# Moving the positions' load to SyncE's queue, and putting the lambda vectors into a buffer of the first chunks

## The chip, the cores and the metric

The kernel runs on one core of a Trainium2 chip. The metric is the device time of one execution in microseconds (us), taken as the median of several runs. The engines of the core are PE (TensorE, matrix products; its weight loads are listed apart as PEld), DVE (VectorE), ACT (ScalarE), POOL (GpSimd) and SP (SyncE, which here only issues DMAs). DMAs can also be issued by ACT and POOL. A queue name such as SPq means the instruction stream of that engine as far as it issues DMAs.

## The reference

One decoder layer on 512 tokens of width 1024, in float32. Cut to what the change is near:

```python
def reference(x, mem, positions, g_mix, w_in, lambda_q1, lambda_k1, lambda_q2, lambda_k2, ...):
    cos, sin = rope_tables(positions, x.dtype)      # angles = positions * 8 frequencies
    u = rms_norm(h, g_mix[l]) @ w_in[l]             # 512 x 1024 @ 1024 x 3072: q, k, v of two mixers
    qa = apply_partial_rope(qa, cos, sin)
    ka = apply_partial_rope(ka, cos, sin)
    lam = (exp(sum(lambda_q1 * lambda_k1)) - exp(sum(lambda_q2 * lambda_k2)) + lam_init)
    ya = diff_attention(qa, ka, va, lam, g_subln[l], lam_init)      # softmax 1 - lam * softmax 2
    yb = stick_breaking_attention(qs, ksb, vs)
    h = h + concatenate([ya, yb]) @ w_out[l]
    h = h + cross_attention(rms_norm(h, g_cross), rms_norm(mem, g_mem), w_xq, w_xkv, w_xo)
    h = h + square(relu(rms_norm(h, g_mlp) @ w_up)) @ w_down
    return rms_norm(h, g_final)
```

The positions feed the rotary tables; the four lambda vectors of 64 numbers feed one scalar, `lam`, that is first used in the softmax of the first mixer.

## The kernel before

Every float32 product is made of three products of halves: each operand is split into `hi` (rounded) and `lo` (the rest), and `mm3` (lines 101 to 104) adds hi·hi, hi·lo and lo·hi in one PSUM tile. ACT makes a `hi` (lines 109, 111), DVE the `lo` (lines 113, 115), for the weights as for the activations. PE is fed by a static order of products that is written out by hand; the other loads and splits are placed around it.

The change touches the start, about the first 36 us. There the input `x` comes in four column blocks `xt[0..3]`, and each of its eight chunks of 128 columns goes through `first_chunk(c)`: PE transposes it into PSUM (line 544), ACT and DVE split it into `A[0][:, c]` and `A[1][:, c]` (lines 111 and 115; the trace calls them `a`). `first_mm(w, c)` then multiplies chunk c with the first 512 columns of `w_in`, into four PSUM tiles (`sc`, `av`), 12 products for each chunk. The loop `for c in range(2, 8, 2)` goes over pairs of chunks. Inside it, `load_x` issues the next block of x on SP, `keep_x` copies the transposed chunks to SBUF on ACT (line 555) and stores them to HBM on SP (line 556), `fetch` issues the next weight load on SP (line 122), and `squares(c)` sums the squares of one block: ACT squares it into `junk`, which has two buffers used in turn (line 572), and DVE reduces that (line 573). In the last round, c = 6, `means` makes of these sums the scale of each token with a chain of tiny DVE instructions of four elements a partition (lines 577 to 582 and, through `rsqrt`, 170 to 175), and chunk 7's `lo` (line 115) stands behind that chain on DVE.

Two small side jobs run beside this. The positions are loaded by POOL (line 532); POOL converts them (line 647) and reduces the angles in a chain of 34 small instructions (lines 649 to 665), ACT takes the sines (lines 668, 669), DVE spreads them (lines 672 to 684) and PE transposes the tables (line 693). The four lambda vectors, each broadcast to 128 partitions of 256 bytes, are loaded by SP into `lv` (line 635); DVE multiplies and sums them (lines 704, 706), ACT takes the exponentials (line 707) and DVE makes `neglam` (lines 708, 709).

The order on PE, and in this part on ACT and DVE, is the one in which the code is written, except that what is written behind `order.close()` (line 697; the lambda arithmetic is) is placed by a scheduler where it expects the inputs. SP's and POOL's order is the scheduler's. Each engine then works strictly in order. DMAs of SP and ACT take eight completion semaphores in turn, so that a DMA also waits for the one that had its semaphore before.

Of the kernel before, what the change touches and what calls it, by code (L numbers as in the profile page):

```python
# [10 lines left out]
F32 = mybir.dt.float32  # L11
# [7 lines left out]
P = 128  # L19
# [43 lines left out]
def tile_decoder_layer(  # L63
# [24 lines left out]
    nc = tc.nc  # L88
# [52 lines left out]
    def fetch(n):  # L141
        while len(loaded) < min(len(stream), n):
            loaded.append(stream[len(loaded)]())

    def take(ahead=2):
        fetch(taken[0] + 1 + ahead)
        taken[0] += 1
        return loaded[taken[0] - 1]
# [39 lines left out]
    def tr_tile():  # L188
        return pp.tile([P, S], F32, tag="tr", bufs=2, name="tr")
# [329 lines left out]
    sp = st.enter_context(tc.tile_pool(name="st", bufs=1))  # L519
# [8 lines left out]
    def load_x(c):  # L528
        nc.sync.dma_start(xt[c], x[:, c * 256:(c + 1) * 256].rearrange("(t p) d -> p t d", p=P))

    pos_i = sp.tile([P, 4], I32, name="pos_i")
    nc.gpsimd.dma_start(pos_i, positions[0].rearrange("(t p) -> p t", p=P))
    lv = sp.tile([P, 4, 64], F32, name="lv")

    qs = [q_tiles() for _ in range(4)] + [None] * 4
    ks = [None] * 8
# [4 lines left out]
    def first_chunk(c):  # L541
        ps = mm_tile() if c % 2 else tr_tile()
        for t in range(4):
            nc.tensor.transpose(ps[:, t * P:(t + 1) * P], xt[c // 2][:, t, (c % 2) * P:(c % 2 + 1) * P], ident)
        split(A[0][:, c, :], A[1][:, c, :], ps, gcol[:, c:c + 1])

        x_ps[c] = ps
# [4 lines left out]
    def keep_x(c):  # L552
        xs = sp.tile([P, 2, S], F32, tag="xs", bufs=2, name="xs")
        for i in range(2):
            nc.scalar.copy(xs[:, i, :], x_ps[c + i])
        nc.sync.dma_start(xdram[:, c:c + 2, :], xs)

    def first_mm(w, c):
        if c < 2:

            for a, b in ((0, 0), (0, 1), (1, 0)):
                for h in range(4):
                    nc.tensor.matmul(q_ps[h], w[a][:, c, h * P:(h + 1) * P], A[b][:, c, :],
                                     start=c == 0 and a + b == 0, stop=False)
            return
        for h in range(4):
            col = slice(h * P, (h + 1) * P)
            mm3(q_ps[h], (w[0][:, c % 2, col], w[1][:, c % 2, col]), (A[0][:, c, :], A[1][:, c, :]), c == 0, c == 7)

    def squares(c):  # L570
        junk = sp.tile([P, 4, 256], F32, tag="junk", bufs=2, name="junk")
        nc.scalar.activation(junk, xt[c], AF.Square, bias=0.0, scale=1.0)
        nc.vector.tensor_reduce(ss4[:, c, :], junk, AX.X, ALU.add)

    def means():
        ss = sp.tile([P, 4], F32, name="ss")
        nc.vector.tensor_reduce(ss, ss4.rearrange("p c t -> p t c"), AX.X, ALU.add)
        nc.vector.tensor_scalar(ss, ss, 1.0 / D, EPS, ALU.mult, ALU.add)
        r = rsqrt(sp, ss, 4, "rsx")
        nc.vector.tensor_copy(rs, r)  # L580
        nc.vector.tensor_scalar(rs8, r, 0.125, None, ALU.mult)
        nc.vector.tensor_scalar(nrs8, r, -0.125, None, ALU.mult)
# [24 lines left out]
    for c in range(2, 8, 2):  # L607
        if c == 4:
            tr = tr_tile()
            nc.tensor.transpose(tr[:, 0:25], grow, ident[:25, :25])  # L610
            nc.vector.tensor_copy(gcol[:, 8:33], tr[:, 0:25])
            nc.vector.tensor_scalar(gcol[:, 32:33], gcol[:, 32:33], 1.0 - LAM_INIT, None, ALU.mult)
        load_x(c // 2)
        keep_x(c - 2)
        fetch(c // 2 + 1)
        w = take(0)
        if c == 2:
            first_mm(w, 0)
        if c == 6:
            squares(2)  # L620
            first_chunk(6)
            squares(3)
            means()
            first_chunk(7)
        else:
            first_chunk(c)
            squares(c // 2 - 1)
            first_chunk(c + 1)
        if c > 2:
            first_mm(w, c - 2)  # L630
        first_mm(w, c - 1)
    keep_x(6)
    w = take(0)
    for i, v in enumerate((lambda_q1, lambda_k1, lambda_q2, lambda_k2)):
        nc.sync.dma_start(lv[:, i, :], v.broadcast_to([P, 64]))
    fetch(5)
# [696 lines left out]
```

## Time and profile before

| | |
|---|---|
| median of 3 runs | 780.06 us (779.12 to 781.5) |
| the profiled execution, its own time | 783.51 us |
| its span in the trace | 781.7 us |
| granted TensorE clock, mean | 0.993 of full speed |
| PE busy in the span | 763.2 us, 98% |
| DVE busy | 516.6 us, 66% |
| ACT busy | 424.8 us, 54% |
| POOL busy | 74.7 us, 10% |

Between the span and the execution's own time lie 1.8 us. The trace gives for each instruction its start, its duration and what its engine waited for before it, in us from the span's start; for a DMA it gives the time at which the issuing engine was busy with it and, apart from that, how long after the issue the data had landed. PE is in work nearly all the time, so what counts is where PE stands idle.

### The profile page before, as it was taken

Reading aid. Unit: us, or ns where it says so; the run is one execution under the profiler, and the core shown is the slowest. Engines: PE = TensorE matmul, PEld = TensorE weight load, DVE = VectorE, ACT = ScalarE, POOL = GpSimd, SP = SyncE. Lnnn points to the kernel's source line nnn. Section 1 sums busy time; section 2 is a strip of 40 time slices with the busy share of each in tenths; the row PEclk is TensorE's granted clock in tenths of the full one; section 3 lists DMA queues with packets and bytes.
Section 4 is the critical chain, followed back from the end, with each engine's and each line's share of the span. In section 5 each row is a group of like instructions: output and inputs, shape, how many; then the busy total and the mean of one; then the engine's idle time right before and its main releaser. Section 6 shows DMA issues by size and latency. Waiting matters only on the chain.

```text
span 781.7 us, 11806 instructions
## 1 busy us (share of the span) xinstructions
PE 763.2 (98%) x4618; PEld 662.0 (85%) x4618; DVE 516.6 (66%) x809; ACT 424.8 (54%) x720; POOL 74.7 (10%) x196
## 2 busy tenths in 40 slices
PE   8999999999898999999999999999999999999996
PEld 7787988778767898888788999889988899889885
DVE  4796665686766664465656989547855586647745
ACT  6657565886845543453535886334733364444622
POOL 6242332311000020000000030000000000000000
PEclk9999999999998999999999999999999999999999
DMA  8466363766643454241560145241333233220302
GB/s 289 162 144 142 82 147 90 169 136 134 182 142 120 124 162 135 80 135 55 162 189 1 51 166 158 81 139 54 109 103 112 81 109 109 99 91 1 135 1 107
DMA packets 88425, 91.61 MB, mean 117 GB/s; under 512 B 3473, under 2 KB 71730, under 8 KB 88114
## 3 DMA queue, kind: packets, MB, share of 16 engines
q1 hardware_dynamic: 84528, 78.39, 32.0%
q0 software_dynamic: 3200, 11.54, 8.1%
q10 hardware_dynamic: 642, 0.93, 0.3%
q8 instruction: 36, 0.59, 0.3%
q14 instruction: 19, 0.16, 0.1%
HBM read 73.03 MB, written 4.19 MB: 99 GB/s over the span
## 4 chain that ended last, share of the span: by engine, by line
PE 87%; ACT 5%; DVE 3%; DMA 3%; issue 2%; POOL 0%; DVEq 0%; SPq 0%; POOLq 0%; ACTq 0%
PE mm L102 14%; PE mm L103 14%; PE mm L104 14%; PE av L102 5%; PE av L104 5%; PE av L103 5%; PE sc L102 4%; PE sc L104 4%; PE sc L103 4%; PE tr L103 4%; PE tr L104 4%; PE tr L102 4%; PE sc L385 2%; PE tr L428 1%; PE av L457 1%
## 5 line engine op out<-in xcount | busy, mean ns | idle before, releaser
L113 DVE TENSOR_TENSOR lo<-raw,hi 128x1024 fp32r<-128x1024 f32 (+1 forms) x73 | 88.2, 1209 | 41.1 <-ACT hi L109 39.9
L109 ACT ACTIVATE hi<-raw 128x1024 fp32r<-128x1024 f32 (+1 forms) x73 | 76.2, 1045 | 63.9 <-PE tr L103 15.2
L109 ACT ACTIVATE hi<-blk 128x1024 fp32r<-128x1024 f32 x40 | 42.5, 1061 | 70.1 <-PE sc L104 48.3
L102 PE MATMUL mm<-a,hi 128*128 128x512 f32 x152 | 64.1, 422 | 3.5 <-DVE resid L493 3.2
L113 DVE TENSOR_TENSOR lo<-blk,hi 128x1024 fp32r<-128x1024 f32 x40 | 48.8, 1221 | 25.9 <-ACT hi L109 25.9
L104 PE MATMUL mm<-a,lo 128*128 128x512 f32 x152 | 61.1, 402 | 0.1
L103 PE MATMUL mm<-a,hi 128*128 128x512 f32 x152 | 61.0, 401 | 0.0
L102 PE MATMUL mm<-b,hi 128*128 128x512 f32 x128 | 50.3, 393 | 0.0
L104 PE MATMUL mm<-b,lo 128*128 128x512 f32 x128 | 50.0, 391 | 0.0
L103 PE MATMUL mm<-b,hi 128*128 128x512 f32 x128 | 49.9, 390 | 0.0
L104 PE MATMUL av<-a,lo 128*128 128x256 f32 (+1 forms) x140 | 41.0, 293 | 0.0
L102 PE MATMUL av<-a,hi 128*128 128x256 f32 (+1 forms) x140 | 40.9, 292 | 0.0
L103 PE MATMUL av<-a,hi 128*128 128x256 f32 (+1 forms) x140 | 40.9, 292 | 0.0
L102 PEld LDWEIGHTS mm<-a,hi 128*128 128x128 f32 x152 | 29.3, 193 | 9.6 <-DVE resid L493 3.7
L102 PE MATMUL tr<-a,hi 128*128 128x256 f32 x128 | 36.2, 283 | 0.0
L104 PE MATMUL tr<-a,lo 128*128 128x256 f32 x128 | 36.2, 283 | 0.0
L103 PE MATMUL tr<-a,hi 128*128 128x256 f32 x128 | 36.2, 283 | 0.0
L104 PEld LDWEIGHTS mm<-a,lo 128*128 128x128 f32 x152 | 29.2, 192 | 7.3 <-DVE lo L113 0.5
L103 PEld LDWEIGHTS mm<-a,hi 128*128 128x128 f32 x152 | 29.4, 194 | 5.6 <-DVE a L113 0.2
L102 PE MATMUL mm<-hi,a 128*128 128x256 f32 x112 | 33.1, 295 | 0.0
L109 ACT ACTIVATE hi<-s 128x1024 fp32r<-128x1024 f32 x16 | 17.0, 1061 | 27.3 <-PE sc L104 14.6
L104 PE MATMUL mm<-hi,a 128*128 128x256 f32 x112 | 31.6, 282 | 0.0
(404 smaller groups left out, 2349.1 us busy)
## 6 DMA issues: line engine op xcount, KB each, us to landing
blk<-in_w_up_dram SPq DMA_DIRECT2D x32, 512.0 KB, 3.7
raw<-in_w_down_dram SPq DMA_DIRECT2D x32, 512.0 KB, 3.2
raw<-in_w_in_dram SPq DMA_DIRECT2D x23, 512.0 KB, 4.5
lo<-raw POOLq DMA_DIRECT2D x20, 512.0 KB, 4.8
raw<-in_w_xkv_dram SPq DMA_DIRECT2D x16, 512.0 KB, 3.8
raw<-in_w_out_dram SPq DMA_DIRECT2D x8, 512.0 KB, 4.6
raw<-in_w_xq_dram SPq DMA_DIRECT2D x8, 512.0 KB, 3.9
raw<-in_w_xo_dram SPq DMA_DIRECT2D x8, 512.0 KB, 4.3
```

Of the source, the lines that this page charges most:

```text
L102: nc.tensor.matmul(o, l[0], r[0], start=first, stop=False)
L103: nc.tensor.matmul(o, l[0], r[1], start=False, stop=False)
L104: nc.tensor.matmul(o, l[1], r[0], start=False, stop=last)
L109: nc.scalar.activation(hi, src, AF.Copy, bias=0.0, scale=scale)
L113: (eng or nc.vector).tensor_tensor(lo, src, hi.bitcast(F32), ALU.subtract)
L385: nc.tensor.matmul(sc[:, h, :n], q[a][own[h], blk], k[b][own[h], :n], start=n_pass == 0, stop=False)
L428: nc.tensor.transpose(tr[:, j, :], self.es[i][:, h, j * P:(j + 1) * P], ident)
L457: nc.tensor.matmul(o[:, cols], vj, w, start=(j == 0 and part == 0), stop=(j == 3 and part == 1))
```

## The change

Two loads are moved; nothing that is computed changes.

```diff
     pos_i = sp.tile([P, 4], I32, name="pos_i")
-    nc.gpsimd.dma_start(pos_i, positions[0].rearrange("(t p) -> p t", p=P))
-    lv = sp.tile([P, 4, 64], F32, name="lv")
...
         if c == 6:
+            nc.sync.dma_start(pos_i, positions[0].rearrange("(t p) -> p t", p=P))
             squares(2)
             first_chunk(6)
             squares(3)
...
     keep_x(6)
     w = take(0)
+    lv = sp.tile([P, 4, 256], F32, tag="junk", bufs=2, name="lv")[:, :, 0:64]
     for i, v in enumerate((lambda_q1, lambda_k1, lambda_q2, lambda_k2)):
         nc.sync.dma_start(lv[:, i, :], v.broadcast_to([P, 64]))
```

The positions (512 integers, 4 bytes to a place) are now loaded by SP. The lambda vectors now lie in the `junk` buffer that `squares(2)` used, so their loads wait for DVE's reduction of that buffer. In the changed kernel line numbers from 534 to 619 are smaller by two, those from 620 to 633 by one, and those behind are the same.

On SP, at the place of the lambda loads, the order before was (in brackets what an instruction waits for: an engine's semaphore, or one of the DMA semaphores HW0 to HW7):

```order
L529 DMA x_117<-in_x_dram 128x4x256 [waits DMAHW5_49]
L635 DMA lv<-in_lambda_q_dram 128x64 [waits DMAHW6_49]
L635 DMA lv<-in_lambda_k_dram 128x64 [waits DMAHW7_49]
L635 DMA lv<-in_lambda_q_dram 128x64 [waits DMAHW0_49]
L635 DMA lv<-in_lambda_k_dram 128x64 [waits DMAHW1_49]
L122 DMA raw<-in_w_in_dram 128x2x512 [waits DMAHW2_49,DVE_49]
L556 DMA xdram<-xs 128x1024 [waits DMAHW3_49,Activation_49]
```

Now the positions stand behind the last block of x:

```order
L529 DMA x_117<-in_x_dram 128x4x256 [waits DMAHW5_49]
L618 DMA pos_i<-in_positions_dram 128x4x1 [waits DMAHW6_49]
L122 DMA raw<-in_w_in_dram 128x2x512 [waits DMAHW7_49,DVE_49]
L554 DMA xdram<-xs 128x1024 [waits DMAHW0_49,Activation_49]
L122 DMA raw<-in_w_in_dram 128x8x128 [waits DMAHW2_49,DMAHW1_49,DVE_49]
```

And the lambda loads stand four weight loads and three stores later on SP, behind the weights for the first `v` columns:

```order
L554 DMA xdram<-xs 128x1024 [waits Activation_49]
L122 DMA raw<-in_w_in_dram 128x4x256 [waits DMAHW7_49,DMAHW5_49,DVE_49]
L635 DMA lv<-in_lambda_q_dram 128x64 [waits DMAHW6_49,DVE_49]
L635 DMA lv<-in_lambda_k_dram 128x64
L635 DMA lv<-in_lambda_q_dram 128x64 [waits DMAHW0_49]
L635 DMA lv<-in_lambda_k_dram 128x64 [waits DMAHW1_49]
L554 DMA xdram<-xs 128x1024 [waits DMAHW2_49,Activation_49]
```

The positions have taken the first place of the lambda loads, and these wait for DVE now. On DVE, the chain of `means` stood alone before (`ss`, `rsx`, `rsx_t` are its tiles):

```order
L170 TENSOR_SCALAR rsx<-ss 128x4 [waits DVE_49]
L172 TENSOR_TENSOR rsx_t<-rsx 128x4 [waits DVE_49]
L174 SCALAR_TENSOR_TENSOR rsx_t<-rsx_t,ss 128x4 [waits DVE_49]
L175 SCALAR_TENSOR_TENSOR rsx<-rsx_t,rsx 128x4 [waits DVE_49]
L172 TENSOR_TENSOR rsx_t<-rsx 128x4 [waits DVE_49]
```

Now the lambda arithmetic stands inside it:

```order
L170 TENSOR_SCALAR rsx<-ss 128x4 [waits DVE_49]
L172 TENSOR_TENSOR rsx_t<-rsx 128x4 [waits DVE_49]
L704 TENSOR_TENSOR lp<-lv 128x128 [waits DMAHW6_49,DMAHW7_49,DMAHW1_49,DMAHW0_49]
L174 SCALAR_TENSOR_TENSOR rsx_t<-rsx_t,ss 128x4 [waits DVE_49]
L706 TENSOR_REDUCE ls<-lp 128x2 [waits DVE_49]
L175 SCALAR_TENSOR_TENSOR rsx<-rsx_t,rsx 128x4 [waits DVE_49]
L172 TENSOR_TENSOR rsx_t<-rsx 128x4 [waits DVE_49]
L708 TENSOR_TENSOR neglam<-ls 128x1 [waits Activation_49]
L174 SCALAR_TENSOR_TENSOR rsx_t<-rsx_t,ss 128x4 [waits DVE_49]
L709 TENSOR_SCALAR neglam<-neglam 128x1 [waits DVE_49]
L175 SCALAR_TENSOR_TENSOR rsx<-rsx_t,rsx 128x4 [waits DVE_49]
```

Four instructions have moved in from earlier places, and the first of them waits for the four lambda loads. Behind this piece, unchanged, come one more round of lines 172 to 175, three copies and chunk 7's `lo`. On ACT the exponential of line 707 moves from before the copies of chunks 4 and 5 to between those of chunks 6 and 7. On POOL the load is gone and the chain is otherwise the same; PE's order is the same throughout.

## Rows read from the trace of the kernel before

**Rows 1.** The page, busy us (share of the span) xinstructions.

```profile
PE 763.2 (98%) x4618; PEld 662.0 (85%) x4618; DVE 516.6 (66%) x809; ACT 424.8 (54%) x720; POOL 74.7 (10%) x196
```

**Rows 2.** Waits of PE, whole span: us in total, times, longest.

```profile
PE mm L102 <- DVE resid L493: 3.2, 1, 3.2
...
PE mm L544 <- DMA x<-in_x_dram: 0.5, 1, 0.5
```

**Rows 3.** DMA issues: KB each, us from issue to landing.

```profile
x<-in_x_dram SPq DMA_DIRECT2D x1, 256.0 KB, 3.0
...
x<-in_x_dram SPq DMA_DIRECT2D x1, 256.0 KB, 5.3
...
lv<-in_lambda_k_dram SPq DMA_DIRECT2D x1, 32.0 KB, 7.1
```

**Rows 4.** Stretches: PE, PEld, DVE, ACT, POOL busy, PEclk, DMA share, GB/s.

```profile
5.00:6.00 1.00, 1.00 (x7) 0.94 (x7) 0.17 (x1) 0.00 (x0) 0.00 (x0) 1.00 0.72 108
6.00:7.00 1.00, 0.59 (x6) 0.32 (x3) 0.19 (x1) 0.91 (x2) 0.00 (x0) 1.00 0.67 161
...
9.00:10.00 1.00, 1.00 (x6) 0.82 (x5) 0.90 (x2) 0.99 (x3) 0.91 (x2) 1.00 1.06 388
```

**Rows 5.** Timeline of POOL: start, us, engine, line, operation [idle before <-releaser].

```profile
2.14 0.99 POOL L532 DMA_DIRECT2D pos_i<-in_positions_dram  x1
...
7.67 0.54 POOL L647 CAST pos<-pos_i 128x4 f32<-128x4 int32 x1 [3.47 <-DMA pos_i<-in_positions_dram]
...
12.28 1.28 POOL L658 TENSOR_TENSOR ang<-ang,kp 128x32 f32<-128x32 f32 x1
...
16.23 0.25 POOL L658 TENSOR_TENSOR ang<-ang,kp 128x32 f32<-128x32 f32 x1
...
22.41 0.29 POOL L665 TENSOR_SCALAR anc<-anc 128x32 f32<-128x32 f32 x1
```

**Rows 6.** Timeline of SP.

```profile
7.51 1.13 SPq L635 DMA_DIRECT2D lv<-in_lambda_q_dram  x1
8.69 0.43 SPq L635 DMA_DIRECT2D lv<-in_lambda_k_dram  x1
...
24.04 0.38 SPq L122 DMA_DIRECT2D raw<-in_w_in_dram  x1
```

**Rows 7.** Timeline of DVE.

```profile
12.23 1.23 DVE L113 TENSOR_TENSOR lo<-raw,hi 128x1024 fp32r<-128x1024 f32 x1 [2.33 <-ACT hi L109]
...
16.24 0.39 DVE L704 TENSOR_TENSOR lp<-lv 128x128 f32<-128x128 f32 x1 [0.25 <-DMA lv<-in_lambda_q_dram]
...
16.67 0.29 DVE L706 TENSOR_REDUCE ls<-lp 128x2 f32<-128x128 f32 x1
...
23.93 1.21 DVE L573 TENSOR_REDUCE ss<-junk 128x4 f32<-128x1024 f32 x1
...
27.59 0.16 DVE L172 TENSOR_TENSOR rsx_t<-rsx 128x4 f32<-128x4 f32 x1
27.78 0.16 DVE L174 SCALAR_TENSOR_TENSOR rsx_t<-rsx_t,ss 128x4 f32<-128x4 f32 x1
...
29.58 0.74 DVE L115 SCALAR_TENSOR_TENSOR a<-mm,gcol,a 128x512 fp32r<-128x512 f32 x1
...
33.95 0.18 DVE L672 TENSOR_TENSOR cs<-cs,rs 128x32 f32<-128x32 f32 x1
...
35.38 0.17 DVE L682 COPY ctok<-cs 128x32 f32<-128x32 f32 x1
```

**Rows 8.** The chain that ended last, 10 to 35 us: start, us, what.

```profile
30.98 0.23 PE sc L103
```

**Rows 9.** Timeline of PE's weight loads.

```profile
35.60 0.58 PEld L693 LDWEIGHTS tr<-ident,ctok 128*128 128x128 f32 x4
```

**Rows 10.** Timeline of ACT and its queue.

```profile
11.13 1.06 ACT L109 ACTIVATE hi<-raw 128x1024 fp32r<-128x1024 f32 x1 [1.14 <-DMA raw<-in_w_in_dram]
...
33.35 0.21 ACT L669 ACTIVATE cs<-anc 128x32 f32<-128x32 f32 x1
```

## Prediction

> **What bounds the kernel now.** I read the page first: PE is busy for 763.2 of 781.7 us [rows 1], so a change counts only where it makes PE wait or ends a wait. The waits of PE come next: the longest, 3.24 us, is late in the first half and has nothing to do with the two loads; the only one at the start that the list shows is 0.54 us for a block of x [rows 2]. Then I looked for what stands closest behind PE where the moved instructions now are: the chain that ended last runs through PE there, product after product. In it the first product with chunk 7's lo begins at 30.98 us [rows 8]. That lo is made by DVE at 29.58 and takes 0.74 us, so it is there at 30.32 [rows 7]: **PE has 0.66 us in hand**. A second place is a little later. The cosine is done on ACT at 33.56 [rows 10], DVE takes it up at 33.95 and ends the cosine table with the instruction from 35.38 to 35.55 [rows 7], and PE loads the first piece of it at 35.60 [rows 9]. So ACT has 0.39 us in hand there, and DVE none worth counting. ACT's chain to the cosine hangs on DVE as well: its copy of chunk 7 waits for that same lo, and a split, a table load and the sine follow in order.
>
> **The load leaves POOL.** POOL loses an issue of 0.99 us [rows 5]; nothing waits for POOL there, and POOL then waits 3.47 us for the data anyway, so the issue itself is worth nothing. What may be worth something is the traffic. While the positions' load is on its way, until 7.67 us, the DMA engines move 108 and 161 GB/s from 5 to 7 us, against 388 from 9 to 10 [rows 4]; the second half of the first x block needs 5.3 us to land, the first half 3.0 [rows 3]. Missing are (388 - 108) + (388 - 161) = 507 GB/s times 1 us, about 0.5 MB or 1.3 us of full rate. Some of that is there because SP itself waited before the next x block; how much is due to the positions the trace doesn't tell. What can be gained is bounded by two waits: PE's 0.54 us [rows 2] and ACT's 1.14 us for the weights at 11.13 [rows 10]. So between 0 and 1.0 us, PE's own work between them taking some; I take the middle, **0.5 us gained**.
>
> **The load arrives on SP.** It takes the first place of the lambda loads, at about 7.5 us. Its issue there costs nothing to what is queued behind it on SP: one issue takes the place of four, so the next weight load can only come earlier. The lambda load at 8.69 landed after 7.1 us, at 15.8 [rows 3, 6], behind the same queue of x and weights, and I give the positions the same time. 512 places of 4 bytes have no row of their own; the range goes from 14.6 (7.51 + 7.1) to 20 us. POOL then starts 8.1 us later than at 7.67; its chain took 15.03 us to 22.70 [rows 5], with stretched instructions beside lo splits in it (one in rows 5), and lo splits lie in the new stretch too. So it ends near **30.9 us**. The sine and cosine were taken at 33.2 to 33.6 [rows 10], so the tables are in time by 2.5 us, and by more if ACT is late itself. Cost 0 as long as the positions land before 18.3 us.
>
> **But the chain now runs beside other work.** Before, POOL was done when the chain of tiny DVE instructions began. What happens when both read SBUF shows at 12.28: an instruction of POOL that takes 0.25 us elsewhere took 1.28 and ended 0.1 us after DVE's lo split of 1.23 us that had begun at 12.23 [rows 5, 7]. The other way round, DVE's product of the lambdas at 16.24 (two tensors of 128 elements) took 0.39 us, while a sum over the same 128 took 0.29; POOL had begun an instruction of 0.25 us at 16.23 [rows 5, 7]. So 0.10 us for each two-input instruction that meets POOL. From 29 to 31 us some 7 of them do (lines 172, 174, 175 and the first neglam): **0.7 us**. Bounds: 0, and 9 times 0.25 = 2.3 us if each waits for a whole instruction of POOL.
>
> The Trainium skill, on the page "SBUF — State Buffer", section "Who interferes with whom", says that a VectorE instruction with two SBUF inputs and a GpSimd instruction that reads SBUF exclude each other, and that the one that starts first holds the port for the whole instruction. The long POOL row beside the lo split agrees; that DVE's short instructions would each wait a whole POOL instruction is the upper bound just given, and no row here shows it for four elements. By it the change would come out slower; that is the second rival below.
>
> **The lambda loads wait.** They need the buffer that `squares(2)` used. Its reduction runs from 23.93 to 25.14 [rows 7]; SP is free at 24.42 [rows 6], so the buffer costs 0.7 us, and the place behind the weights the rest. Behind them on SP stands the store of chunks 6 and 7, which waits for ACT's copy of chunk 7, and that for DVE's lo, so it is not held up by the issues. An issue took 0.43 to 1.13 us [rows 6]; the queue is shorter at 25 us than at 7.5, so I take 0.43 and a step of 0.48: the fourth starts at 25.17 + 3 x 0.48 = 26.6. A load into an idle machine landed in 3.0 us with 256 KB [rows 3], of which 0.7 us are its bytes at 388 GB/s, so I estimate 2.3 us for 32 KB: **28.9 us**. DVE gets to the product of the lambdas at about 27.75, behind the instruction of 27.59 [rows 7]. It stands still for **1.1 us**, and with it the chain of means. Bounds: 0 (landed in time), and 2.6 us (a first step of 1.18, steps of 0.52, landing in 3.0: 30.4).
>
> **The lambda arithmetic itself** now lies in that chain: 0.39 and 0.29 us [rows 7], and two of one element, which I put at the 0.16 of four elements [rows 7]: 1.0 us. The chain steps 0.19 us for an instruction of 0.16, so independent ones fill small gaps; I take **0.8 us**, bounds 0.5 and 1.1. The exponential on ACT waits for nothing else at that moment. What the four instructions leave behind, the first at 16.24 us, gives nothing: PE runs on there.
>
> **Sum.** DVE's lo of chunk 7 is late by 0.8 + 1.1 + 0.7 = 2.6 us. PE first waits 2.6 - 0.66 = 1.9 us for it at 30.98; the cosine comes 2.6 us later on ACT and takes another 0.3 at the tables, so PE is late by 2.6 - 0.39 = 2.2 us in all. I see nothing later that gives this back: the scores, the rotary products and the weight buffers that follow all start from PE's results. With the 0.5 us from the start: **+1.7 us**. The profiled execution would go from 783.51 to 785.2; its span is 781.7, with 1.8 us around it that the change doesn't touch. The profiled execution lies 3.45 us above the median of the runs, and I apply the difference to the median: 780.06 + 1.7 = **781.8 us**.
>
> **The rivals.**
> First, the covers hold: the lambdas land by 27.75, POOL meets few instructions, D (the delay of the lo) is 0.8, of which 0.4 gets through, and the start gives it back: 780.06 + 0.4 - 0.4 = 780.1. For it speaks that 32 KB is little; against it, that four issues one after another are needed and that DVE waits for the last.
> Second, slower: POOL's chain and DVE's chain take turns, and each of 9 instructions waits 0.25 us. D is 0.8 + 1.1 + 2.3 = 4.2, PE is late by 3.8, less 0.5: 783.4. It decides from about 0.15 us per instruction, since 0.3% is 2.34 us and 2.34 + 0.5 + 0.39 - 1.9 = 1.3 us is left for 9. Speaking for it: POOL's chain leaves little room between its instructions, 34 and a conversion in 15.03 us. Against it: the one meeting that a row shows cost 0.10.
> Third, the positions come too late: 4-byte pieces may be slow behind full queues. It decides where POOL's chain ends after the cosine's new time, 33.35 + 2.6, that is for a landing after 20.9 us; each us beyond costs one. At 23 us: 783.9.
> Fourth, the start gives its full 1.0 us and the covers hold: 780.06 - 1.0 + 0.3 = 779.4. Faster by a measurable amount would need more than both waits hold.
> That the loads don't move as written is excluded by the order of the changed kernel.
>
> **How the numbers follow.** Forecast 0.40, first rival 0.25, second 0.22, third 0.06, fourth 0.07. A measurement of this kernel tells about 0.3%, 2.34 us, from no change, so the forecast and the first rival count as the same. Slower: the second and third and the upper edge of the forecast, 0.30; faster 0.04, mostly for runs that scatter (779.12 to 781.5 before); same 0.66. The likeliest case alone spans 780.9 to 782.5. The range for 8 in 10 goes from 779.5 (just above the fourth rival) to 784.0, which takes in the second rival and not all of the third.
>
> **What would show it.** Right: DVE idle before the lambda product until about 28.9 us, released by a DMA; chunk 7's lo at about 32 us; PE idle for about 2 us before line 103's product at 31 to 33 us, and again 0.3 us before the cosine table; POOL's chain from about 15.8 to 31 us. Wrong: the lambda product without a wait; PE without a gap at 31 us; instructions of lines 172 to 175 at 0.16 us throughout (no meeting with POOL) or near 0.4 (rival two); ACT waiting for POOL before the sine (rival three); the DMA rate from 5 to 7 us as low as before, which takes the 0.5 us away. A gap of PE that is filled later by a shorter wait elsewhere would make the sum wrong even with each step right.

## The result and the profile after

The changed kernel takes **787.86 us** (median of 6, 784.35 to 788.99); the kernel before, run beside it, 781.55 (779.12 to 782.15). The ratio is **1.0067 [1.0050, 1.0085]**: slower, and outside the predicted range of 779.5 to 784.0. In four later comparisons the same kernel gave 1.0061, 1.0045, 1.0039 and 1.0040. The profiled execution is the fastest of the six: it took 784.35 us, with a span of 782.6 and a mean granted clock of 0.995.

PE's busy time has not moved; its waits have. The page's busy line of the kernel after, beside [rows 1]:

```profile
PE 762.5 (97%) x4618; PEld 661.2 (84%) x4618; DVE 516.3 (66%) x809; ACT 425.2 (54%) x720; POOL 73.2 (9%) x195
```

The waits of PE in the kernel after (us in total, times, longest), where [rows 2] had 3.2 us and no wait for `a`:

```profile
PE mm L102 <- DVE resid L493: 2.7, 1, 2.7
PE sc L103 <- DVE a L115: 2.4, 1, 2.4
...
PE tr L103 <- DMA lo<-raw: 1.3, 1, 1.3
```

The new wait of 2.4 us is the one for chunk 7's `lo`. Its origin begins in the timeline of SP, again of the kernel after:

```profile
6.73 0.70 SPq L618 DMA_DIRECT2D pos_i<-in_positions_dram  x1
...
24.06 0.34 SPq L635 DMA_DIRECT2D lv<-in_lambda_q_dram  x1
...
25.39 0.43 SPq L635 DMA_DIRECT2D lv<-in_lambda_k_dram  x1
```

The DMA view of the kernel after has the landing of the last of these:

```profile
lv<-in_lambda_k_dram SPq DMA_DIRECT2D x1, 32.0 KB, 4.4
```

And the timeline of DVE, after, shows who waits:

```profile
21.67 1.23 DVE L113 TENSOR_TENSOR lo<-raw,hi 128x1024 fp32r<-128x1024 f32 x1 [1.61 <-ACT hi L109]
22.82 1.21 DVE L571 TENSOR_REDUCE ss<-junk 128x4 f32<-128x1024 f32 x1
...
26.51 0.18 DVE L172 TENSOR_TENSOR rsx_t<-rsx 128x4 f32<-128x4 f32 x1
29.88 0.29 DVE L704 TENSOR_TENSOR lp<-lv 128x128 f32<-128x128 f32 x1 [3.19 <-DMA lv<-in_lambda_k_dram]
...
32.03 0.74 DVE L115 SCALAR_TENSOR_TENSOR a<-mm,gcol,a 128x512 fp32r<-128x512 f32 x1
```

The reduction of line 571 frees the lambda loads' buffer at 24.03, and SP issues the first of them at 24.06. The last is issued at 25.39 us and lands 4.4 us later. DVE, which is through with line 172 at 26.69, stands for 3.19 us, and chunk 7's `lo` begins at 32.03 where it began at 29.58 [rows 7]. That is 2.45 us later than before. PE takes that over, as its timeline shows (kernel after):

```profile
32.83 0.50 PE L103 MATMUL sc<-a,hi 128*128 128x512 f32 x1 [2.42 <-DVE a L115]
...
37.92 0.60 PE L693 MATMUL tr<-ident,ctok 128*128 128x128 f32 x4
```

The product of line 693 is 2.1 us later than in PE's timeline of before:

```profile
35.82 0.60 PE L693 MATMUL tr<-ident,ctok 128*128 128x128 f32 x4
```

POOL's chain moved and did no harm (timeline of POOL, after). It ends at 29.04 us, before the lambda product starts, so it never runs beside the rest of DVE's chain. It has the stretched instructions beside lo splits that [rows 5, 7] showed.

```profile
14.76 0.19 POOL L647 CAST pos<-pos_i 128x4 f32<-128x4 int32 x1 [11.59 <-DMA pos_i<-in_positions_dram]
...
21.84 1.17 POOL L658 TENSOR_TENSOR ang<-ang,kp 128x32 f32<-128x32 f32 x1
...
28.74 0.30 POOL L665 TENSOR_SCALAR anc<-anc 128x32 f32<-128x32 f32 x1
```

The first microseconds have more traffic, where [rows 4] had 108 and 161 GB/s (stretches of after, last columns: DMA share, GB/s):

```profile
5.00:6.00 1.00, 1.00 (x7) 0.94 (x7) 0.17 (x1) 0.00 (x0) 0.00 (x0) 1.00 0.91 313
6.00:7.00 1.00, 1.00 (x9) 1.00 (x8) 0.18 (x1) 0.90 (x2) 0.00 (x0) 1.00 1.03 329
```

**The clock.** What I had not read before is in the stretches by windows (PE, PEld, DVE, ACT, POOL busy, then PEclk). The kernel before has a 3.24 us wait [rows 2]; the kernel after has one of 2.69 us at the same product. PE's timelines show where they end, first before, then after:

```profile
236.75 0.79 PE L102 MATMUL mm<-a,hi 128*128 128x512 f32 x1 [3.24 <-DVE resid L493]
```

```profile
238.59 0.50 PE L102 MATMUL mm<-a,hi 128*128 128x512 f32 x1 [2.69 <-DVE resid L493]
```

The stretches of the kernel before around it:

```profile
235.00:240.00 5.00, 3.25 (x8) 2.58 (x9) 2.50 (x3) 3.23 (x5) 0.00 (x0) 0.54 0.19 75
240.00:245.00 5.00, 5.00 (x19) 3.97 (x18) 3.90 (x9) 3.23 (x5) 0.19 (x1) 0.77 0.65 209
```

Those of the kernel after:

```profile
235.00:240.00 5.00, 2.31 (x9) 1.51 (x8) 1.36 (x2) 1.43 (x3) 0.00 (x0) 0.93 0.54 196
240.00:245.00 5.00, 5.00 (x18) 4.00 (x17) 3.38 (x6) 4.15 (x7) 0.00 (x0) 0.73 0.35 98
```

Read as time at 1.2 GHz in place of 2.4 (twice the share that is missing): before 2 x (0.46 + 0.23) x 5 = 6.9 us, after 2 x (0.07 + 0.27) x 5 = 3.4 us. Of the 6.9 us, 4.6 lie ahead of 240 us, so they begin near 235.4, 1.3 us before the wait ends, and there the low clock costs PE nothing. Of the other 5.5 us, and of the 3.4, half is lost, as PE is in work. So the profile of before happened to hold a long slow stretch and that of after a short one, and the two spans, 781.7 and 782.6, differ by less than the kernels do. The runs have to be read by their means.

For that I split each execution's span into a part **lost to the clock**, span x (1 - mean granted clock), and the rest, the **part at full clock**. About 2.0 us of the loss are the end of the kernel, where PE has no products any more (the profiles of two kernels below, e7 and e8, have no other stretch at 1.2 GHz, and these kernels lose 2.1 and 2.0 in the mean); differences between kernels are free of that. A low clock inside a wait counts as lost too, some 0.7 us in the profile of before, so the split is rough by as much. The first row gives the two parts themselves, the others their difference from the kernel before. Means in us, each beside the kernel before in the same comparison (29, 33 and 29 executions; 776.47 + 3.47, 777.29 + 3.62, 777.01 + 3.42):

| kernel | executions | ratio to before | full clock | lost |
|---|---|---|---|---|
| changed, first six | 6 | 1.0067 | 779.14 | 6.16 |
| changed, again (e3) | 6 | 1.0061 | +2.9 | +1.8 |
| changed, twice more (e6, e6b) | 14 | 1.0045, 1.0039 | +1.8 | +1.2 |
| changed, once more (e11) | 9 | 1.0040 | +2.1 | +1.1 |
| positions alone (e1) | 12 | 1.0012 | +0.9 | +0.1 |
| lambda loads alone (e2) | 12 | 1.0029 | +2.4 | -0.2 |
| changed, lambda arithmetic behind (e4) | 12 | 1.0003 | +0.5 | -0.4 |
| changed, gap of PE filled (e5) | 12 | 1.0034 | +2.7 | +0.2 |
| before, wait at 235 us filled (e7) | 11 | 0.9978 | -0.3 | -1.5 |
| e4 and the filling of e7 (e8) | 12 | 0.9989 | +0.5 | -1.4 |
| changed, the filling of e7 (e9) | 8 | 1.0038 | +2.5 | +0.4 |
| changed, loads of own rows (e10) | 10 | 1.0011 | +0.4 | -0.1 |

Over all 35 executions of the changed kernel and all 91 of the kernel before, the change costs 779.14 - 776.94 = **2.2 us at full clock** and 5.04 - 3.51 = **1.5 us lost to the clock**, with standard errors of 0.2 and 0.3 us. The mean clock was 0.992 or lower in 7 of the 35 and in none of the 91.

### The profile page after: what moved, and what is told of

Its sections match the earlier page's. It is cut to its first block, busy times and chain, and to the rows that moved or that the text cites. A ratio compares the mean times of both kernels' runs of the same rounds, so it can differ in the third digit from the quotient of the medians.

```text
span 782.6 us, 11801 instructions
## 1 busy us (share of the span) xinstructions
PE 762.5 (97%) x4618; PEld 661.2 (84%) x4618; DVE 516.3 (66%) x809; ACT 425.2 (54%) x720; POOL 73.2 (9%) x195
## 4 chain that ended last, share of the span: by engine, by line
PE 85%; ACT 5%; DVE 4%; DMA 3%; issue 2%; SPq 0%; POOL 0%; DVEq 0%; POOLq 0%; ACTq 0%
PE mm L102 14%; PE mm L103 14%; PE mm L104 14%; PE av L102 5%; PE av L103 5%; PE av L104 5%; PE tr L103 4%; PE tr L104 4%; PE tr L102 4%; PE sc L103 4%; PE sc L104 4%; PE sc L102 4%; PE sc L385 2%; PE tr L428 1%; PE av L457 1%
```

## The experiments

My theory after the result: the lambda loads land late, DVE waits for them inside the chain that chunk 7's `lo` stands behind, PE waits for that, and the clock takes more. Rivals: the positions' load on SP (or POOL's later chain) costs the time; the arithmetic itself does; or something away from the start.

**One part of the change each.** e1 moves the positions only, e2 the lambda buffer only; e3 is the changed kernel beside them.

Against the changed kernel, e1 has `lv` at its old place again:

```diff
+    lv = sp.tile([P, 4, 64], F32, name="lv")
...
-    lv = sp.tile([P, 4, 256], F32, tag="junk", bufs=2, name="lv")[:, :, 0:64]
```

And e2 has the positions' load on POOL again:

```diff
+    nc.gpsimd.dma_start(pos_i, positions[0].rearrange("(t p) -> p t", p=P))
...
-            nc.sync.dma_start(pos_i, positions[0].rearrange("(t p) -> p t", p=P))
```

> Only the positions move to SyncE; the lambda vectors keep a buffer of their own. Theory A (the lambda product on VectorE waits for late loads inside the chain of means, TensorE then waits 2.4 us for chunk 7's lo, and the clock that is granted after such a wait costs the rest): no wait at chunk 7's lo, the DMA rate from 5 to 7 us stays near 320 GB/s, ratio 0.997 to 1.001. Rival B (the positions' 4-byte pieces on SyncE's queue, or the later angle chain on GpSimd, cost the time): the slowdown stays, ratio 1.004 to 1.008.

> Only the lambda vectors move into the buffer of the first chunks; the positions stay on GpSimd. Theory A: the wait of VectorE at the lambda product is there, TensorE is late by about 2 us at the cosine table, and the first microseconds keep their slow DMA stretch from 5 to 7 us, so 1.005 to 1.010, at least as slow as the change. Rival B: 0.998 to 1.002, the slowdown gone.

> The changed kernel itself once more, for the granted clock of each execution and a second profile. Theory A: executions fall into two groups, mean clock near 0.995 with a span near 783 us and near 0.990 with a span near 786.5; a profile of the second group shows a stretch of 1.2 GHz behind the wait at 30 to 33 us that the first profile does not have. Rival C (the clock falls elsewhere, behind the wait for x before the output projection near 235 us, for longer): a second profile shows full clock from 30 to 60 us and a longer stretch of 1.2 GHz near 240. Ratio 1.005 to 1.009 by both.

Measured: e1 782.68 us, 1.0012 [0.9999, 1.0026]; e2 783.85, 1.0029 [1.0019, 1.0038]; e3 786.15, 1.0061 [1.0044, 1.0077]. The waits of e2 at DVE's lambda product and at PE's chunk 7:

```profile
DVE lp L704 <- DMA lv<-in_lambda_k_dram: 2.7, 1, 2.7
...
PE sc L103 <- DVE a L115: 2.5, 1, 2.5
```

The same two of e3:

```profile
DVE lp L704 <- DMA lv<-in_lambda_k_dram: 3.1, 1, 3.1
...
PE sc L103 <- DVE a L115: 2.9, 1, 2.9
```

The timelines of e3, first DVE, then SP, show the first lambda load right behind the reduction of its buffer, as in the profile of after, but both 1.1 us later:

```profile
23.92 1.21 DVE L571 TENSOR_REDUCE ss<-junk 128x4 f32<-128x1024 f32 x1
...
30.89 0.29 DVE L704 TENSOR_TENSOR lp<-lv 128x128 f32<-128x128 f32 x1 [3.09 <-DMA lv<-in_lambda_k_dram]
```

```profile
25.16 0.34 SPq L635 DMA_DIRECT2D lv<-in_lambda_q_dram  x1
```

The positions alone can't be told from no change by their ratio, though their part at full clock is 0.9 us longer; e1's profile has neither wait, though POOL waits 12.6 us for its positions. The lambda loads alone make the waits, and most of the loss at full clock, 2.4 us where e3 has 2.9. What they don't make alone is the loss to the clock: e2 has none in the mean.

**The same change without the wait in the chain.** e4 leaves both loads where the change put them and writes the lambda arithmetic directly behind the loads in the code. The order on DVE is then the written one, and the product stands behind chunk 7's `lo`.

```diff
         nc.sync.dma_start(lv[:, i, :], v.broadcast_to([P, 64]))
+    lp = sp.tile([P, 2, 64], F32, name="lp")
+    nc.vector.tensor_tensor(lp, lv[:, 0:4:2, :], lv[:, 1:4:2, :], ALU.mult)
...
+    nc.vector.tensor_scalar(neglam, neglam, -LAM_INIT, None, ALU.add)
     fetch(5)
```

> The changed kernel, loads as in it, but the lambda product, sum and neglam stand on VectorE behind chunk 7's lo, where it was idle for 1.9 us before. Theory A: chunk 7's lo comes before TensorE needs it, no wait at 30 us, the start keeps its gain of about 1 us in VectorE and ScalarE: ratio 0.997 to 1.001. Rival B (the late loads or the positions themselves): 1.004 to 1.008.

Measured 781.90 us, 1.0003 [0.9991, 1.0014]. DVE's timeline of e4:

```profile
29.09 0.74 DVE L115 SCALAR_TENSOR_TENSOR a<-mm,gcol,a 128x512 fp32r<-128x512 f32 x1
30.14 0.29 DVE L637 TENSOR_TENSOR lp<-lv 128x128 f32<-128x128 f32 x1 [0.31 <-DMA lv<-in_lambda_k_dram]
```

The `lo` is 0.5 us earlier than in the kernel before, PE has no wait for it, and the loss is gone, with every load as slow as before (one landed after 4.8 us). So it is the place of the waiting instruction that costs, not the loads' traffic and not the positions.

**Is the clock's part due to the gap?** e5 fills PE's gap: 30 identity products stand between the first and the second product of chunk 7.

```diff
-    first_mm(w, 7)
+    for h in range(4):
...
+        nc.tensor.matmul(q_ps[h], hi, A[0][:, 7, :], start=False, stop=False)
+        if h == 0:
+            wps = mm_tile()
+            for _ in range(30):
+                nc.tensor.matmul(wps[:, :P], identb, identb, start=True, stop=True)
+        nc.tensor.matmul(q_ps[h], hi, A[1][:, 7, :], start=False, stop=False)
+        nc.tensor.matmul(q_ps[h], lo, A[0][:, 7, :], start=False, stop=True)
```

> The changed kernel with 30 products of the identity put into TensorE's wait for chunk 7's lo; they write a PSUM tile that nobody reads. The late lambda loads and the late lo stay. Theory A (the wait costs twice: about 2.8 us as a delay, and about 2 us more by the clock that falls to 1.2 GHz after it): no stretch of 1.2 GHz before 60 us, the part of the span at full clock stays near 779.2 us, the part lost to the clock falls from 5.2 to 6.2 us to what the kernel before loses (3.5), ratio 1.003 to 1.0045. Rival C (what is lost to the clock comes from the wait near 235 us alone): lost part and ratio as in the change, 1.005 to 1.008. Rival D (the delay itself is larger in most executions than the profile shows): ratio 1.005 to 1.008, at a full-clock part above 781.

> The changed kernel for another profile. Theory A: a span of 785 us or more comes with two stretches of 1.2 GHz ahead of the last 10 us, one behind 33 us and one behind 236 us; a span near 783 with one of them.

> The changed kernel for another profile, expectation as for the look before: a span of 785 us or more shows both stretches of 1.2 GHz, a span near 783 one.

Measured: e5 785.54 us, 1.0034 [1.0018, 1.0049]; the changed kernel beside it 785.70, 1.0045 [1.0029, 1.0062], and 784.80, 1.0039 [1.0021, 1.0058]. The times don't tell the three apart. In the split e5 lost 3.79 us to the clock where the changed kernel lost 4.82, which agrees with the theory, though it is only about twice the scatter of these means; and its part at full clock was 0.9 us longer, so nothing was won. Why it is longer is not shown. In e5's profile PE's old wait near 235 us is 3.65 us, and 2.6 to 3.1 in the five profiles of the changed kernel, so the time may have come back as a longer wait there. In e5's profile PEclk is 1.00 from 30 to 40 us, and 0.50 from 240 to 245; in e6 and e6b it fell between 30 and 40 us and was 1.00 from 235 to 245. Here are the stretches from 30 to 40 us of e11, the changed kernel once more:

```profile
30.00:35.00 5.00, 2.40 (x9) 1.59 (x8) 2.72 (x16) 2.12 (x4) 0.00 (x0) 0.87 0.11 44
35.00:40.00 5.00, 5.00 (x22) 4.01 (x21) 4.84 (x17) 3.26 (x5) 0.00 (x0) 0.79 0.49 169
```

The profile of e9, the changed kernel with products placed before the wait at 235 us, shows **both stretches in one execution**:

```profile
30.00:35.00 5.00, 2.20 (x7) 1.48 (x6) 2.73 (x16) 1.83 (x4) 0.00 (x0) 0.82 0.05 19
35.00:40.00 5.00, 5.00 (x22) 3.96 (x21) 4.04 (x16) 3.56 (x5) 0.00 (x0) 0.84 0.42 148
...
240.00:245.00 5.00, 3.70 (x9) 2.93 (x10) 2.94 (x4) 3.23 (x5) 0.00 (x0) 0.66 0.12 45
```

In both, 3.4 us at 1.2 GHz stand at the end of the new wait. In e11's timeline of PE the products of 512 columns then begin 0.43 us apart, not 0.23:

```profile
33.08 0.50 PE L103 MATMUL sc<-a,hi 128*128 128x512 f32 x1 [2.60 <-DVE a L115]
33.42 0.39 PE L104 MATMUL sc<-a,lo 128*128 128x512 f32 x1
33.65 0.58 PE L102 MATMUL sc<-a,hi 128*128 128x512 f32 x1
34.03 0.63 PE L103 MATMUL sc<-a,hi 128*128 128x512 f32 x1
34.45 0.63 PE L104 MATMUL sc<-a,lo 128*128 128x512 f32 x1
```

**The old wait at 235 us.** If a long wait of PE costs clock, filling the one that was there all along must gain. e7 is the kernel *before* with 34 identity products ahead of that wait; e8 is e4 with them, e9 the changed kernel with them, and e11 the changed kernel beside e8 and e9.

```diff
             ps = mm_tile()
+            if n == 2:
+                wps = tr_tile()
+                for _ in range(34):
+                    nc.tensor.matmul(wps[:, :P], identb, identb, start=True, stop=True)
             run(proj_n(A, ps, S))
```

> The kernel before, with 34 products of the identity put into TensorE's wait for the rows of x near 235 us, into a PSUM tile that nobody reads. Theory A (a wait of 2.4 us or more lets the clock fall, whatever the kernel): the part lost to the clock falls from 3.5 us to the 1.7 to 2.5 us that the last microseconds cost, the full-clock part stays at 776.5, ratio 0.997 to 0.9995. Rival C' (the clock falls there for another reason than TensorE's idleness): nothing changes, 0.9995 to 1.001.

> The changed kernel with two edits: the lambda arithmetic is written directly behind the lambda loads (as in the run that put it behind chunk 7's lo on DVE), and 34 identity products of 128 columns stand on PE before the third product group of the output projection, where PE waits 2.6 to 3.6 us near 235 us. Theory (the loss is one new PE wait at 31 to 34 us with what the clock takes after it, and the two places are independent): the run with the arithmetic behind gave 776.99 us at full clock and 3.06 lost to the clock, the run of the kernel before with the products took the loss from 3.62 to 2.12; so 0.998 of the kernel before, about 1.5 us faster than the run with the arithmetic behind alone, no granted clock of 1.2 GHz before the last 10 us. Rival (moving the loads costs something else that the clock at 235 covered, or the filling only works in the old order): 1.000 or above.

> The changed kernel with the 34 identity products before the third product group of the output projection alone; the new wait of 2.4 to 3.1 us near 33 us stays. Theory (two long waits of PE, each of which can be followed by a stretch at 1.2 GHz; the changed kernel's slow executions are those with both): the part lost to the clock falls from 4.4 to 6.2 us to about 3.5, the time at full clock stays at 779, so 782.5 + 1.8 = 784.3 or 1.7 below the changed kernel of the same call, 1.003 of before, and the profile shows 1.2 GHz at about 34 us or not at all, never at 235. Rival (the loss to the clock belongs to the wait at 33 us alone): no better than the changed kernel, within 0.5 us.

> The changed kernel unchanged, beside the other three on the same chip. Expected as before: 1.004 to 1.007, PE waits of 2.4 to 3.1 us near 33 us and 2.6 to 3.1 near 240. Theory (both waits can each take the clock): mean granted clock of the executions between 0.989 (two stretches) and 0.995 (one). Rival (one stretch in each execution): 0.995 throughout.

Measured: e7 780.86 us, **0.9978 [0.9969, 0.9988]**; e8 781.21, 0.9989 [0.9978, 1.0001]; e9 784.86, 1.0038 [1.0018, 1.0058]; e11 785.47, 1.0040 [1.0023, 1.0056]. The stretch of e7 that had 0.54 and 0.77 in the kernel before:

```profile
235.00:240.00 5.00, 3.94 (x19) 3.13 (x18) 3.07 (x4) 3.24 (x5) 0.00 (x0) 1.00 0.10 43
240.00:245.00 5.00, 5.00 (x23) 4.07 (x22) 3.79 (x11) 3.24 (x5) 0.19 (x1) 1.00 0.68 216
```

e7's gain is the clock's: 1.5 us less lost, with 34 products more to do. e8 loses as little, so both places can be mended in the changed kernel, which then isn't measurably faster than before; e7 has the lowest ratio here. e9 failed my expectation: a wait of 1.85 us was left behind the products, and the clock fell behind it all the same. PE's timeline of e9:

```profile
241.30 0.71 PE L102 MATMUL mm<-a,hi 128*128 128x512 f32 x1 [1.85 <-DVE resid L493]
```

In its eight executions it lost 0.7 us less than e11, too little to tell.

**Why do 32 KB take 4.4 us to land?** e10 lets each of the four loads read 128 different rows of 256 bytes of `x` in place of one lambda row 128 times, and so leaves out the lambda numbers.

```diff
-    for i, v in enumerate((lambda_q1, lambda_k1, lambda_q2, lambda_k2)):
-        nc.sync.dma_start(lv[:, i, :], v.broadcast_to([P, 64]))
+    for i in range(4):
+        nc.sync.dma_start(lv[:, i, :], x[i * P:(i + 1) * P, 0:64])
```

> The changed kernel, but each of the four loads of 128 rows of 256 bytes reads 128 different rows of x in place of one lambda row 128 times; the lambda numbers are so left out, all instructions and sizes stay. Theory (the landing 4.4 to 4.8 us after the issue, 512 pieces between 25.8 and 29.7 us, goes by the number of pieces): landing again 4.4 to 4.8 us, DVE waits 3.0 to 3.3 us, time within 0.1% of the changed kernel in this call. Rival (all pieces of a load reading the same 256 bytes is what is slow): landing 2.5 to 3.0 us, DVE waits about 1.5 us, PE waits about 0.8 us in place of 2.4 to 3.0 and the clock holds there, 782 to 783 us.

Measured 782.37 us, 1.0011 [0.9996, 1.0027], against 1.0040 for the changed kernel beside it. The theory failed, and the rival's numbers are what came. e10's DMA issues:

```profile
lv<-in_x_dram SPq DMA_DIRECT2D x4, 32.0 KB, 2.3
```

The waits of e10 at its lambda product and at PE's chunk 7:

```profile
DVE lp L704 <- DMA lv<-in_x_dram: 0.8, 1, 0.8
...
PE sc L103 <- DVE a L115: 0.6, 1, 0.6
```

The same pieces, as many and as large, land in 2.3 us (2.0 to 2.6) when they read different rows of `x`. e10 reads another tensor too, so the runs don't separate the repeated reading of one row from the place of the lambda tensors in memory. The stretches (last columns: DMA share, GB/s) tell it too; e11, with the broadcast loads:

```profile
27.00:28.00 1.00, 1.00 (x6) 0.79 (x6) 0.29 (x2) 0.00 (x0) 0.78 (x3) 1.00 0.13 31
28.00:29.00 1.00, 1.00 (x6) 0.82 (x5) 0.00 (x0) 0.00 (x0) 0.77 (x4) 1.00 0.13 32
29.00:30.00 1.00, 1.00 (x6) 0.83 (x5) 0.00 (x0) 0.00 (x0) 0.55 (x2) 1.00 0.14 31
```

The same stretches of e10:

```profile
27.00:28.00 1.00, 1.00 (x6) 0.83 (x5) 0.37 (x3) 0.00 (x0) 0.75 (x4) 1.00 0.34 74
28.00:29.00 1.00, 1.00 (x6) 0.82 (x5) 0.74 (x5) 0.13 (x1) 0.83 (x4) 1.00 0.00 0
```

Reading one row over and over, the loads trickle at some 31 GB/s with the DMA engines busy for an eighth; reading own rows they are through before 28 us.

The Trainium skill, page "DMA: Bandwidth & Descriptors", section "Anatomy of one DMA — SWDGE (gpsimd) path", fits a DMA that GpSimd issues by about 2.0 us plus its bytes at 436 GB/s, by which 32 KB would take an estimated 2.1 us. These loads are issued by SP. The 2.3 us of e10 are near that, the 3.6 to 4.9 us of the broadcast loads behind the weights in these runs are not; the measurement decides.

## Why the prediction was wrong

The place and the chain were right; sizes were not, and one term was missing. Point by point, as the prediction put it:

- *"PE has 0.66 us in hand"* and the chain from DVE's lambda product over chunk 7's `lo` to line 103 and line 693: right. PE's new wait stands where it was forecast.
- *"The load leaves POOL ... 0.5 us gained"* (0 to 1.0): the DMA rate from 5 to 7 us rose to 313 and 329 GB/s in the profile of after, against 108 and 161 [rows 4]. In this profile ACT's wait for its weights fell from 1.14 us [rows 10] to 0.42, and DVE came to the lambda product 1.06 us earlier, at 26.69. But that is one profile: in the four later ones of the same kernel (e3, e6, e6b, e11), at 226 to 325 GB/s, ACT waits 1.2 to 1.5 us there, and DVE comes between 0.4 us earlier and 0.1 us later than before. And in e4's profile, where chunk 7's `lo` is 0.5 us earlier than before, PE's later wait for the weights' `lo` is 1.5 us in place of 1.0, so *"I see nothing later that gives this back"* need not hold for a gain at the start. e1, with the positions on SP and nothing else changed, is no faster.
- *"The load arrives on SP"*, cost 0: right. Forecast was 15.8 us for the landing and 30.9 for the end of POOL's chain; it was 14.76 and 29.04.
- *"0.7 us"* for DVE instructions that meet POOL's: none met. POOL was done when DVE got its lambdas.

  The Trainium skill's rule on the port ("SBUF — State Buffer", section "Who interferes with whom"), that a DVE instruction with two SBUF inputs contends with a GpSimd instruction that reads SBUF, stood beside the prediction's second rival. It is seen at POOL's 1.17 us instruction at 21.84, which ends 0.1 us after DVE's lo split of 21.67 to 22.90; in the chain it had no occasion.
- *"I estimate 2.3 us for 32 KB: 28.9 us"*, a DVE wait of 1.1 us (0 to 2.6): **mis-sized**. The loads landed 4.4 us after the issue and DVE waited 3.19 us, beyond the upper bound; in the four later profiles it waited 2.8 to 3.2. The 2.1 us too few are the landing. DVE's earlier arrival did not lengthen the wait, for the loads came earlier with it: the first is issued 0.03 us after the reduction that frees their buffer. In e3, where DVE is 1.1 us later than in the profile of after, that issue is 1.1 us later as well, and DVE waits 3.09 us. e10 shows the estimate to be good for loads of different rows, 2.3 us and 0.8 of wait. I took a load of distinct data for the price of a broadcast one; the row of 7.1 us [rows 3], which I put down to the queue ahead, was the only broadcast one that I had used.
- *"The lambda arithmetic ... 0.8 us"*: from the end of line 172 or the wait to the `lo` it is 32.03 - 29.88 = 2.15 us, before 29.58 - 27.75 = 1.83. So 0.3, under the lower bound of 0.5: the gaps in the chain of tiny instructions hid most of it.
- *"Chunk 7's lo is late by 2.6 us"*: 2.45 in the profile, near by errors that cancel (wait +2.1, arithmetic -0.5, POOL -0.7, start -1.06). In the four later profiles, without that start, it is 2.7 to 3.5 us late.
- *"PE is late by 2.2 us in all ... +1.7"*: line 693 is 2.1 us late in the profile, and 3.6 to 4.4 in the four later ones, the low clock included. The mean cost at full clock is 2.2 us, 0.5 above the sum. That it is so near is luck. In e10, where the loads land as estimated, PE waits 0.6 us where the sum had 1.9, and the cost at full clock is 0.4 us where it had 1.7: the sum had the landing too small, and the arithmetic and POOL's part too large.
- **The steps that failed** are two. One is the landing of the broadcast loads, put at 2.3 us and measured at 4.4; with 2.3 (e10) no loss can be told. The other is missing: the sum priced a wait of PE at its length and put the clock at nothing. In the mean of 35 executions 1.5 us more are lost to the granted clock, in the first six 2.65. In e4 and e10, where the wait is gone or short, this loss is gone too. The row to read was beside [rows 2]: the 3.24 us wait of the kernel before goes with 6.9 us at 1.2 GHz. I named that wait only to set it aside.
- Of the 6.1 us between 781.8 and 787.86, 1.5 are the kernel before, which was 780.06 in the runs shown and 781.55 beside the changed kernel; 0.5 are the full clock and 2.65 the clock. The rest is a median of six executions that lies above their mean (spans 786.1 and 785.3) and other scatter.

What stays open: which wait is followed by 1.2 GHz, and for how long, in a given execution. Five profiles of the changed kernel have one stretch each, one near 240 us and four near 34. That the executions at a mean clock of 0.992 or less hold both is inferred from e9's profile, not seen in one of theirs. Nor is it shown why e2, with the same new wait and in its profile 3.4 us at 1.2 GHz behind it, lost no more to the clock in the mean than the kernel before: that the new wait alone costs the 1.5 us is not shown.

## What to carry to other kernels

An instruction that waits for a DMA belongs behind the last short chain that the busiest engine needs, not inside it: the same loads cost 0.3 to 0.7% in one place on DVE and nothing measurable behind that chain. When a change makes a wait on PE, look up what the clock does after the waits that the kernel already has, and put that beside the length of the wait. Price a DMA by a row of the same kind, with the same source pattern, and not by one of the same bytes.

## What was not expected of the hardware

- Loads that read one row of 256 bytes into 128 partitions landed 3.6 to 4.9 us after the issue, at 31 GB/s and a DMA share of 0.13 (e11); loads of 128 different rows of that size, of another tensor, landed in 2.0 to 2.6 us.
- A wait of PE of 2.6 us (e11) was followed, 0.6 us after its end, by 3.4 us at 1.2 GHz, and one of 1.85 behind small products by 3.4 (e9). With one of 3.24 us went 6.9, which began 1.3 us before its end (before). Others of 2.4 (e4, at 235 us), 2.24 (e8, behind small products) and 3.1 us (e3, at 235) were followed by none. So length alone doesn't decide it, and 34 small products ahead of the wait made the kernel before faster by 0.22% [0.12, 0.31].
